# One value scale per head group, applied in the copies; the prompt's neighbourhood planes made one step later

## The chip, the cores and the metric

One core of one Trainium2 chip runs the whole kernel. The metric is the device time of one execution in microseconds (us); what is compared are medians of several executions. The profile and the trace come from one execution, recorded by the hardware profiler. Its engines are called PE (TensorE, the matrix engine), PEld (its weight loads), DVE (VectorE), ACT (ScalarE), POOL (GpSimd) and SP (SyncE, which here only issues DMAs).

## The reference

One encoder layer is applied to two inputs, x_prompt (1024 tokens) and x_sample (512 tokens), both 1024 wide:

```
xn = RMSNorm(x);  z = xn @ W_in -> q_A k_A v_A q_B k_B v_B gate_A gate_B
o_A = softmax(q_A k_A^T / 8) v_A     # 8 query heads share 2 key/value heads; RMS-normed, rotated q and k
o_B = softmax(q_B k_B^T / 8 + bias) v_B   # 8 heads, a clamped 8 x 16 window on a token grid 64 wide
mix = (sigmoid(gate_A) * (o_A @ W_pA) + sigmoid(gate_B) * (o_B @ W_pB)) @ W_out
x = x + mix;  x = x + relu(RMSNorm(x) @ W_up)^2 @ W_down;  y = RMSNorm(x)
```

Everything is float32, and the outputs must be close to a float32 computation.

## The kernel before

**Precision.** A float32 product is made of three matmuls on operands that are split into a high and a low part (mm3, lines 242 to 245). In the prompt's attention, the probabilities and the values are kept as two float16 planes, high and low, of a number that was scaled into the range of float16. The probabilities are scaled by the constant PSC. The values are scaled column by column; the scales are worked out from the weights, as a bound on the largest value that a column can give (value_scales, lines 180 to 204).

**Stages.** The sample (s0) goes first, then the prompt (s1), each through: the projections of branch A for key/value group 0 (phR), grouped attention of that group (phA), the same for group 1, neighbourhood attention (phB, branch B), the output projections (phG). The profiled execution has them at, in us: s0 projections 0 to 50 and 93 to 127, grouped attention 50 to 93 and 127 to 170, neighbourhood attention 170 to 320, outputs 320 to 390; s1 projections 390 to 460 and 575 to 650, grouped attention 460 to 575 and 650 to 760, neighbourhood attention 760 to 1065, outputs 1065 to 1250. The MLP of both inputs fills the rest.

**Order.** A scheduler puts each engine's instructions in a row from the order of the code and its own estimate of lengths; some instructions are pinned to the order of the code. At run time each engine works its row off strictly, waiting for semaphores. The matmuls of the gates are cut into pieces ("fill", outputs gpss) and are put between the others wherever the code calls fill.pull, so that PE has work while other engines prepare its operands. DMAs are issued mostly by SP, in a row as well.

**The value scales before.** During the sample's neighbourhood attention, a block of 128 weight columns (raw, one of three shared load buffers called rawvs here) is loaded per step. DVE takes the absolute value (aw, line 197), PE multiplies it with a matrix of the norm's weights (gm) in eight matmuls (line 200), which gives the 128 sums on every partition; DVE adds a tiny number (line 202), takes the inverse (sv, line 203), and ACT's queue writes the row to DRAM (vsc). This is done for five blocks. The prompt's stages read vsc back: broadcast over partitions as svb and svv for the projections (lines 667 to 669), as a column inv for grouped attention (lines 862 to 867) and as iv for neighbourhood attention (lines 1041 to 1047).

**The uses before.** In the prompt's projections, values() lets DVE scale the projected values of branch B (vs, line 712), ACT round them to the high plane and DVE subtract for the low one (vt). rotate() does the same for branch A's values with DVE (line 796), ACT, and POOL for the difference (line 802). In grouped attention, s_tile() takes the inverse of the row sum (rl, line 891, DVE), multiplies it by PSC (rc, line 893, POOL), and makes the planes hl of the probabilities.

**Neighbourhood attention of the prompt.** There are 32 units (8 heads by 4 column blocks), one per step of a loop; fill is pulled twice a step. s_unit() makes a unit's scores in two halves (matmuls sbs, line 1153; both halves lie in one PSUM tile). Per half, DVE adds the bias and mask (bms, made by POOL) and takes the row's maximum in one instruction, which the trace names msbs and sbss (line 1155); ACT takes the exponential (pbs, line 1159); DVE the inverse sum (rsbs, line 1162); POOL multiplies it by PSC (line 1167); ACT makes the high plane (hbs, line 1170) and DVE the low one (line 1171). SP issues a DMA that transposes both planes into bhs (line 1176). There are three buffers of hbs, one per half, and three of bhs. Two steps after the scores, v_unit() multiplies bhs with the values (obs, line 1220), and ACT and DVE scale the result back by iv (lines 1227 and 1228, output os_B).

## Time and profile before

| what | us |
|---|---|
| median of three runs | 2134.73 |
| fastest of the three | 2132.63 |
| the profiled execution's own time | 2130.55 |
| its span in the trace | 2128.7 |
| POOL busy | 351.5 (17%) |
| ACT busy | 1138.2 (53%) |

The span is what the trace covers from first to last instruction; the 1.85 us beside it belong to the start and end of the execution. The mean granted clock of PE is 0.996. A row of a group of instructions names the line, the engine, the operation, what it writes and reads, and minimum, median and maximum in ns. A row of waits names who waited, for whom, the us in total, how many times, and the longest. An event has its start and length, and in brackets how long the engine stood idle before it and what released it.

### The profile page before, as it was taken

Reading aid. Unit: us, or ns where it says so; the run is one execution under the profiler, and the core shown is the slowest. Engines: PE = TensorE matmul, PEld = TensorE weight load, DVE = VectorE, ACT = ScalarE, POOL = GpSimd, SP = SyncE. Lnnn points to the kernel's source line nnn. Section 1 sums busy time; section 2 is a strip of 40 time slices with the busy share of each in tenths; the row PEclk is TensorE's granted clock in tenths of the full one; section 3 lists DMA queues with packets and bytes.
Section 4 is the critical chain, followed back from the end, with each engine's and each line's share of the span. In section 5 each row is a group of like instructions: output and inputs, shape, how many; then the busy total and the mean of one; then the engine's idle time right before and its main releaser. Section 6 shows DMA issues by size and latency. Waiting matters only on the chain.

```text
span 2128.7 us, 31427 instructions
## 1 busy us (share of the span) xinstructions
PE 2078.9 (98%) x10559; PEld 1784.9 (84%) x10559; DVE 1498.4 (70%) x2848; ACT 1138.2 (53%) x2352; POOL 351.5 (17%) x588
## 2 busy tenths in 40 slices
PE   9999899999999999999999999999999999999998
PEld 8887778987797777776788999999999988888887
DVE  6675777778767855667772877778777777659563
ACT  5664454657636755566531566666565633434352
POOL 3332330432242222332101200003000000000000
PEclk9999999999999999999999999999999999999999
DMA  6445647634525556655772666478544799688561
GB/s 189 135 125 155 181 151 260 214 83 103 116 59 127 119 123 130 163 125 133 196 246 102 209 197 200 154 247 210 159 148 157 260 354 341 214 277 275 176 198 69
DMA packets 446582, 376.94 MB, mean 177 GB/s; under 512 B 169158, under 2 KB 384083, under 8 KB 446420
## 3 DMA queue, kind: packets, MB, share of 16 engines
q1 hardware_dynamic: 404471, 307.00, 49.4%
q10 hardware_dynamic: 36268, 50.88, 7.1%
q0 software_dynamic: 5680, 17.04, 2.9%
q8 instruction: 83, 1.36, 0.3%
q14 instruction: 80, 0.65, 0.1%
HBM read 263.62 MB, written 85.79 MB: 164 GB/s over the span
## 4 chain that ended last, share of the span: by engine, by line
PE 49%; DVE 1%; issue 1%; DMA 0%; POOL 0%; ACT 0%; POOLq 0%; ACTq 0%; DVEq 0%
PE dn L243 7%; PE dn L245 7%; PE dn L244 7%; PE uc L243 2%; PE uc L244 2%; PE ud L244 2%; PE ud L243 2%; PE ud L245 2%; PE uc L245 2%; PE ua L245 2%; PE ua L244 2%; PE ua L243 2%; PE ops L244 1%; PE ops L243 1%; PE ops L245 1%; PE ub L244 1%
## 5 line engine op out<-in xcount | busy, mean ns | idle before, releaser
L245 PE MATMUL dn<-wd,al 128*128 128x512 f32 (+1 forms) x624 | 242.3, 388 | 0.0
L244 PE MATMUL dn<-wd,ah 128*128 128x512 f32 (+1 forms) x624 | 242.3, 388 | 0.0
L243 PE MATMUL dn<-wd,ah 128*128 128x512 f32 (+1 forms) x624 | 242.3, 388 | 0.0
L1524 ACT ACTIVATE ah<-ar 128x512 fp32r<-128x512 f32 x168 | 104.4, 627 | 201.8 <-PE dn L244 181.0
L1525 DVE TENSOR_TENSOR al<-ar,ah 128x512 fp32r<-128x512 f32 x168 | 115.1, 693 | 74.6 <-ACT ah L1524 66.6
L245 PEld LDWEIGHTS dn<-wd,al 128*128 128x128 f32 x624 | 117.1, 188 | 24.4
L243 PEld LDWEIGHTS dn<-wd,ah 128*128 128x128 f32 x624 | 117.1, 188 | 24.1
L244 PEld LDWEIGHTS dn<-wd,ah 128*128 128x128 f32 x624 | 117.1, 188 | 24.1
L880 DVE TENSOR_REDUCE nms<-ss 128x1 f32<-128x1024 f32 (+1 forms) x96 | 99.5, 1038 | 12.0 <-PE ss L878 11.6
L883 ACT ACTIVATE ps<-ss,nms 128x1024 f32<-128x1024 f32 (+1 forms) x96 | 93.0, 970 | 24.1 <-DVE nms L880 9.3
L243 PE MATMUL gpss<-xs_0h,w_gs 128*128 128x512 f32 x256 | 102.8, 402 | 2.1 <-DVE ptls L919 1.3
L228 POOL TENSOR_TENSOR rs_f<-ms_f,mhalf 128x1 f32<-128x1 f32 x6 | 4.0, 667 | 590.7 <-DVE ms_f L224 590.7
L245 PE MATMUL gpss<-xs_0h,w_gs 128*128 128x512 f32 x256 | 100.8, 394 | 0.2 <-DVE w_gs L238 0.2
L244 PE MATMUL gpss<-xs_0l,w_gs 128*128 128x512 f32 x256 | 100.8, 394 | 0.0
L1524 ACT ACTIVATE A<-S 128x512 fp32r<-128x512 f32 x128 | 76.1, 624 | 30.9 <-DVE S L1587 26.5
L1525 DVE TENSOR_TENSOR A<-S,A 128x512 fp32r<-128x512 f32 x128 | 84.5, 686 | 3.8 <-ACT A L1524 3.8
L1643 ACT ACTIVATE c<-c 128x384 f32<-128x384 f32 x97 | 50.7, 524 | 67.9 <-DVE c L1642 67.9
L243 PE MATMUL uc<-B,A 128*128 128x384 f32 x256 | 85.6, 334 | 0.2 <-ACT s L1659 0.2
L243 PE MATMUL ud<-B,A 128*128 128x384 f32 x256 | 85.6, 334 | 0.0
L245 PE MATMUL ud<-B,A 128*128 128x384 f32 x256 | 85.5, 334 | 0.0
L244 PE MATMUL ud<-B,A 128*128 128x384 f32 x256 | 85.5, 334 | 0.0
L244 PE MATMUL uc<-B,A 128*128 128x384 f32 x256 | 85.5, 334 | 0.0
(393 smaller groups left out, 6340.8 us busy)
## 6 DMA issues: line engine op xcount, KB each, us to landing
ar<-ud SPq DMA_DIRECT2D x120, 512.0 KB
br<-in_w_mlp_down_dram SPq DMA_DIRECT2D x72, 512.0 KB
rawu<-in_w_mlp_up_dram SPq DMA_DIRECT2D x64, 512.0 KB
ud<-c ACTq DMA_DIRECT2D x128, 192.0 KB
raw_gs<-in_w_in_dram SPq DMA_DIRECT2D x32, 512.0 KB
zgs<-sgs ACTq DMA_DIRECT2D x48, 256.0 KB
ud<-cs SPq DMA_DIRECT2D x64, 192.0 KB
vss<-vds SPq DMA_DIRECT2D x256, 32.0 KB
```

The source lines that it names most:

```text
L228: nc.gpsimd.tensor_tensor(r[:, :n], m[:, :n], mhalf[:, :n], op=ALU.pow)
L243: nc.tensor.matmul(out, ah, bh, start=start, stop=False, **kw)
L244: nc.tensor.matmul(out, ah, bl, start=False, stop=False, **kw)
L245: nc.tensor.matmul(out, al, bh, start=False, stop=stop, **kw)
L880: nc.vector.tensor_reduce(nm_, s, axis=AX.X, op=ALU.max, negate=True)
L883: nc.scalar.activation(p, s, AF.Exp, bias=nm_, accum_out=l)
L1524: nc.scalar.activation(hi, src, AF.Copy)
L1525: nc.vector.tensor_tensor(lo, src, hi.bitcast(F32), op=ALU.subtract)
L1643: nc.scalar.activation(t, t, AF.Relu)
```

## The change

It has four parts.

1. There is one scale for each of four groups of columns (branch A's two key/value heads, and heads 0 to 3 and 4 to 7 of branch B) instead of one per column. It is the sum over the rows of the weights of the largest absolute weight of a row in that group, times the norm's weight. DVE finds the row maxima in five reductions; a single matmul of 128x4 against a constant matrix adds them over the partitions. All is done in the sample's second projection, and the scales stay on the chip in svs; vsc and the DMAs that wrote and read it are gone. The columns of svs are used as a per-partition scalar.
2. In the prompt's projections ACT scales while it copies from PSUM, and DVE makes the low plane from PSUM in one instruction (values, rotate).
3. In grouped attention of the prompt DVE scales the row sum by 1/PSC ahead of its inverse; POOL's multiply is gone, and so is one link of the chain.
4. In the prompt's neighbourhood attention the inverse sums, the planes and the transposes of a unit are a function of their own, planes(), called at the start of the next step. DVE scales both halves' sums in one instruction and inverts them in another; POOL's two multiplies are gone.

```diff
@@ value_scales
-        for b, off in enumerate((640, 1792, 1920, 2048, 2176)):
...
-            nc.sync.dma_start(rv, win[:, off : off + P].rearrange("(k p) c -> p k c", p=P))
-            yield
...
-            nc.vector.scalar_tensor_tensor(aw, rv, -1.0, rv, op0=ALU.mult, op1=ALU.max)
...
-            for k in range(NC8):
-                nc.tensor.matmul(pt, gm[:, k, :], aw[:, k, :], start=(k == 0), stop=(k == NC8 - 1))
...
-            nc.vector.tensor_scalar(sv, pt, 1e-30, None, op0=ALU.add)
-            nc.vector.reciprocal(sv, sv)
-            nc.scalar.dma_start(vsc[:, b * P : (b + 1) * P], sv[0:1, :])
...
+        blocks = ((640, 2, 0), (1792, 1, 0), (1792, 1, 1), (2048, 1, 0), (2048, 1, 1))
...
+        for b in range(3):
+            load(b)
+        yield
+        for b, (off, nh, kb) in enumerate(blocks):
...
+            nc.vector.tensor_reduce(
+                dst.rearrange("p h k -> p k h") if nh == 2 else dst,
+                rv.rearrange("p k (h d) -> p k h d", d=HD) if nh == 2 else rv,
+                axis=AX.X,
+                op=ALU.max,
+                apply_absolute_value=True,
+            )
+            if b + 3 < 5:
+                load(b + 3)
+            if b < 4:
+                yield
...
+        nc.vector.tensor_tensor(top, top, ga.to_broadcast([P, 4, NC8]), op=ALU.mult)
+        nc.vector.tensor_reduce(svs[:, 8:12], top, axis=AX.X, op=ALU.add)
+        yield
+        pt = mm("vs")[:, 0:4]
+        nc.tensor.matmul(pt, ones, svs[:, 8:12], start=True, stop=True)
+        nc.vector.tensor_scalar(svs[:, 4:8], pt, 1e-30, None, op0=ALU.add)
+        nc.vector.reciprocal(svs[:, 0:4], svs[:, 4:8])
+        nc.vector.tensor_scalar(svs[:, 4:8], svs[:, 4:8], 1.0 / PSC, None, op0=ALU.mult)
@@ values
-                        nc.vector.tensor_tensor(vs, zv4, svv.rearrange("p (h d) -> p h d", d=HD), op=ALU.mult)
-                        nc.scalar.activation(vt[:, :, 0:HD], vs, AF.Copy)
-                        nc.vector.tensor_tensor(vt[:, :, HD:P], vs, vt[:, :, 0:HD], op=ALU.subtract)
+                        sv = svs[:, 2 + g : 3 + g]
+                        nc.scalar.activation(vt[:, :, 0:HD], zv4, AF.Copy, scale=sv)
+                        nc.vector.scalar_tensor_tensor(
+                            vt[:, :, HD:P], zv4, sv, vt[:, :, 0:HD], op0=ALU.mult, op1=ALU.subtract
+                        )
@@ rotate
-                            nc.vector.tensor_tensor(vr, z[:, 320:384], svb, op=ALU.mult)
...
-                            nc.scalar.activation(hi, vr, AF.Copy)
-                            nc.gpsimd.tensor_tensor(lo, vr, hi if tt >= NP else hi.bitcast(F32), op=ALU.subtract)
+                            sv = svs[:, g : g + 1]
+                            nc.scalar.activation(hi, z[:, 320:384], AF.Copy, scale=sv)
+                            nc.vector.scalar_tensor_tensor(
+                                lo, z[:, 320:384], sv, hi if tt >= NP else hi.bitcast(F32),
+                                op0=ALU.mult, op1=ALU.subtract,
+                            )
@@ grouped attention, s_tile
-                    nc.vector.tensor_scalar(inv, inv, PSC, None, op0=ALU.mult)
-                    nc.vector.reciprocal(inv, inv)
+                inv = svs[:, 4 + g : 5 + g] if ND else None
...
-                    nc.vector.reciprocal(rl, l)
...
-                    nc.gpsimd.tensor_scalar(rlc, rl, PSC, 1.0, op0=ALU.mult, op1=ALU.mult)
+                    nc.vector.tensor_scalar(l, l, 1.0 / PSC, None, op0=ALU.mult)
+                    nc.vector.reciprocal(rlc, l)
...
-                    nc.gpsimd.tensor_scalar(pn, p[:, 0 : NP * P], rl, PSC, op0=ALU.mult, op1=ALU.mult)
+                    nc.gpsimd.tensor_scalar(pn, p[:, 0 : NP * P], rlc, 1.0, op0=ALU.mult, op1=ALU.mult)
@@ neighbourhood attention, s_unit and planes
-                    nc.vector.reciprocal(rl[:, x : x + 1], l[:, x : x + 1])
...
-                    nc.gpsimd.tensor_scalar(rlc, rl[:, x : x + 1], PSC, 1.0, op0=ALU.mult, op1=ALU.mult)
...
-                    nc.scalar.activation(h2[:, :, 0, :], pv3, AF.Copy, scale=rlc)
...
+            def planes(u):
...
+                nc.vector.tensor_scalar(l[:, 0:2], l[:, 0:2], 1.0 / PSC, None, op0=ALU.mult)
+                nc.vector.reciprocal(rl[:, 0:2], l[:, 0:2])
...
+                for hf in range(2):
...
+                    nc.scalar.activation(h2[:, :, 0, :], pv3, AF.Copy, scale=r_)
                     nc.vector.scalar_tensor_tensor(
-                        h2[:, :, 1, :], pv3, rlc, h2[:, :, 0, :], op0=ALU.mult, op1=ALU.subtract
+                        h2[:, :, 1, :], pv3, r_, h2[:, :, 0, :], op0=ALU.mult, op1=ALU.subtract
                     )
...
                     nc.sync.dma_start_transpose(
...
@@ v_unit
-                    nc.scalar.activation(t, o[HD:P], AF.Copy, scale=iv[HD:P, h : h + 1])
...
+                    nc.scalar.activation(t, o[HD:P], AF.Copy, scale=svs[HD:P, 6 + h // 4 : 7 + h // 4])
...
@@ the loop over the units
+                if JN == 1 and 0 < i <= n:
+                    planes(units[i - 1])
                 if i < n:
                     s_unit(units[i])
...
-                if i >= 3:
-                    next(vsg, None)
```

How the rows of the engines change is shown at three places. Numbers after a name tell buffers apart; sbss1_2_1_0 is the prompt's head 2, column block 1, half 0.

DVE in the prompt's neighbourhood attention, around the units (2, 1) and (2, 2), before (ISA is the reduction of the scores, with its second part that reads the maximum out; hbs are the low planes, os_Bs an output):

```order
L1155 ISA sbss1_2_1_0_9804,msbs1_2_1_9797<-sbs1_2_1_9795,bms1_2_1_0_9800 128x384
L1155 ISA msbs1_2_1_9797 128x1
L1155 ISA sbss1_2_1_1_9818,msbs1_2_1_9797<-sbs1_2_1_9795,bms1_2_1_1_9814 128x384
L1155 ISA msbs1_2_1_9797 128x1
L1162 RECIPROCAL rsbs1_2_1_9799<-ssbs1_2_1_9798 128x1
L1171 SCALAR_TENSOR_TENSOR hbs1_2_1_0_9809<-pbs1_2_1_9796,rsbs1_2_1_9799,hbs1_2_1_0_9809 128x3x128
L1162 RECIPROCAL rsbs1_2_1_9799<-ssbs1_2_1_9798 128x1
L1155 ISA sbss1_2_2_0_9895,msbs1_2_2_9890<-sbs1_2_2_9888,bms1_2_1_0_9800 128x384
L1155 ISA msbs1_2_2_9890 128x1
L1171 SCALAR_TENSOR_TENSOR hbs1_2_1_1_9823<-pbs1_2_1_9796,rsbs1_2_1_9799,hbs1_2_1_1_9823 128x3x128
L1228 SCALAR_TENSOR_TENSOR os_Bs1_1_0_9883<-obs1_1_0_9877,ivs1_8935,ot_Bs1_1_0_9882 64x512
```

The same place in the changed kernel:

```order
L1166 ISA sbss1_2_1_0_9590,msbs1_2_1_9583<-sbs1_2_1_9581,bms1_2_1_0_9586 128x384
L1166 ISA msbs1_2_1_9583 128x1
L1166 ISA sbss1_2_1_1_9597,msbs1_2_1_9583<-sbs1_2_1_9581,bms1_2_1_1_9593 128x384
L1166 ISA msbs1_2_1_9583 128x1
L1184 TENSOR_SCALAR ssbs1_2_1_9584<-ssbs1_2_1_9584 128x2
L1185 RECIPROCAL rsbs1_2_1_9585<-ssbs1_2_1_9584 128x2
L1192 SCALAR_TENSOR_TENSOR hbs1_2_1_0_9664<-pbs1_2_1_9582,rsbs1_2_1_9585,hbs1_2_1_0_9664 128x3x128
L1192 SCALAR_TENSOR_TENSOR hbs1_2_1_1_9668<-pbs1_2_1_9582,rsbs1_2_1_9585,hbs1_2_1_1_9668 128x3x128
L1166 ISA sbss1_2_2_0_9679,msbs1_2_2_9674<-sbs1_2_2_9672,bms1_2_1_0_9586 128x384
L1166 ISA msbs1_2_2_9674 128x1
L1245 SCALAR_TENSOR_TENSOR os_Bs1_1_0_9656<-obs1_1_0_9650,svs_95,ot_Bs1_1_0_9655 64x512
L1166 ISA sbss1_2_2_1_9684,msbs1_2_2_9674<-sbs1_2_2_9672,bms1_2_1_1_9593 128x384
```

The inverse of the first half, which stood between a unit's planes and reductions, is gone from there; one multiply and one inverse for both halves stand ahead of both low planes, and both low planes stand ahead of the next unit's first reduction here.

DVE at the start of the sample's second projection, before (ms_As is the mean square that POOL takes the root of, ts the normed queries and keys):

```order
L224 TENSOR_SCALAR ms_As0_1_0_1292<-ssAs0_1_0_1286 128x5
L789 SCALAR_TENSOR_TENSOR ts0_1_0_1296<-zs0_1_0_1260,rs_As0_1_0_1294,gtab_93 128x64 x5
L805 TENSOR_TENSOR vhls0_1_1257<-zs0_1_0_1260,vhls0_1_1257 128x64
L224 TENSOR_SCALAR ms_As0_1_1_1345<-ssAs0_1_1_1339 128x5
L789 SCALAR_TENSOR_TENSOR ts0_1_1_1349<-zs0_1_1_1313,rs_As0_1_1_1347,gtab_93 128x64 x5
L805 TENSOR_TENSOR vhls0_1_1257<-zs0_1_1_1313,vhls0_1_1257 128x64
L819 TENSOR_TENSOR ts0_1_0_1296<-ts0_1_0_1296,rts0_1_0_1258 128x320
L826 TENSOR_TENSOR rrs0_1_0_1308<-ts0_1_0_1296,us0_1_0_1304 128x320
```

And in the changed kernel:

```order
L207 TENSOR_REDUCE vtop_1262<-rawvs0_1263 128x8x2
L247 TENSOR_SCALAR ms_As0_1_0_1303<-ssAs0_1_0_1297 128x5
L207 TENSOR_REDUCE vtop_1262<-rawvs1_1265 128x4
L811 SCALAR_TENSOR_TENSOR ts0_1_0_1307<-zs0_1_0_1271,rs_As0_1_0_1305,gtab_93 128x64 x5
L207 TENSOR_REDUCE vtop_1262<-rawvs2_1267 128x4
L829 TENSOR_TENSOR vhls0_1_1257<-zs0_1_0_1271,vhls0_1_1257 128x64
L247 TENSOR_SCALAR ms_As0_1_1_1362<-ssAs0_1_1_1356 128x5
L811 SCALAR_TENSOR_TENSOR ts0_1_1_1366<-zs0_1_1_1330,rs_As0_1_1_1364,gtab_93 128x64 x5
L829 TENSOR_TENSOR vhls0_1_1257<-zs0_1_1_1330,vhls0_1_1257 128x64
L219 SCALAR_TENSOR_TENSOR gc_1258<-gc_1258 128x8
```

Three of the five reductions of weights (vtop) now stand among the first tiles' norm and rotation, the first of them ahead of the first mean square.

SP's row in the same stage, before (raw_gs are the loads of gate weights):

```order
L268 DMA raw_gs0_2304_4_0_1455<-in_w_in_dram 128x8x128
L268 DMA raw_gs0_2304_5_0_1621<-in_w_in_dram 128x8x128
L268 DMA raw_gs0_2304_6_0_1692<-in_w_in_dram 128x8x128
L220 DMA biases_97<-shifted_96 128x768
L742 DMA rts0_1_0_1258<-in_rope_dram 128x128
L742 DMA rts0_1_1_1311<-in_rope_dram 128x128
L742 DMA rts0_1_2_1364<-in_rope_dram 128x128
L220 DMA biases_97<-shifted_96 128x768
L742 DMA rts0_1_3_1461<-in_rope_dram 128x128
L268 DMA raw_gs0_2304_7_0_1820<-in_w_in_dram 128x8x128
```

And in the changed kernel:

```order
L196 DMA rawvs0_1263<-in_w_in_dram 128x8x128
L196 DMA rawvs1_1265<-in_w_in_dram 128x4x256
L196 DMA rawvs2_1267<-in_w_in_dram 128x4x256
L243 DMA biases_98<-shifted_97 128x768
L184 DMA gc_1258<-in_norm_mix_g_dram 128x8x1
L764 DMA rts0_1_0_1269<-in_rope_dram 128x128
L196 DMA rawvs3_1323<-in_w_in_dram 128x4x256
L196 DMA rawvs4_1326<-in_w_in_dram 128x4x256
L764 DMA rts0_1_1_1328<-in_rope_dram 128x128
L764 DMA rts0_1_2_1382<-in_rope_dram 128x128
L291 DMA raw_gs0_2304_4_0_1474<-in_w_in_dram 128x8x128
L764 DMA rts0_1_3_1480<-in_rope_dram 128x128
```

The five loads of value weights stand ahead of the gate weights 4 to 7 and use the same three buffers.

More of the change, by code (lines that the diff above doesn't have):

```diff
@@ L115, in encoder @@
     gtab = cst.tile([P, 5, HD], F32, name="gtab")
-    mhalf = cst.tile([P, 48], F32, name="mhalf")
+    mhalf = cst.tile([P, 8], F32, name="mhalf")
+    svs = cst.tile([P, 40], F32, name="svs")
     nc.vector.memset(mhalf, -0.5)
@@ L119, in encoder @@
     biases = dram.tile([8, 16, 8, 16, 48], F32, name="biases")
-    vsc = dram.tile([1, 640], F32, name="vsc")
     def row_bcast(dst, src, n, rep=1):
@@ L188, in value_scales @@
[L188 to L204 removed]
+        ones = pool.tile([P, P], F32, tag="vone", name="vone", bufs=1)
@@ new lines, in value_scales, with load @@
+        nc.gpsimd.memset(ones, D**0.5 / VTOP)
+        top = pool.tile([P, 4, NC8], F32, tag="vtop", name="vtop", bufs=1)
+        blocks = ((640, 2, 0), (1792, 1, 0), (1792, 1, 1), (2048, 1, 0), (2048, 1, 1))
+        raws = {}
+        def load(b):
+            off, nh, kb = blocks[b]
+            ncol = P if nh == 2 else 256
+            raw = rawp.tile([P, 1024], F32, tag="raw", name=f"rawvs{b}")
+            raws[b] = raw.rearrange("p (k c) -> p k c", c=ncol)
+            nc.sync.dma_start(
+                raws[b],
+                win[kb * 512 : kb * 512 + 1024 * P // ncol, off : off + ncol].rearrange("(k p) c -> p k c", p=P),
+            )
@@ L665, in run @@
                 if ND:
-                    svb = ph.tile([P, HD], F32, tag="svb", name=f"svb{N}_{g}", bufs=1)
-                    nc.sync.dma_start(svb, vsc[:, g * HD : g * HD + HD].to_broadcast([P, HD]))
-                    svv = ph.tile([P, 4 * HD], F32, tag="svv", name=f"svv{N}_{g}", bufs=1)
-                    nc.sync.dma_start(svv, vsc[:, P + g * 256 : P + g * 256 + 256].to_broadcast([P, 256]))
                     vpl = vps.tile([P, ND, 2, HD], F16, tag="vp", name=f"vpl{N}_{g}", bufs=1)
+                vsg = value_scales(ph) if first and g == 1 else iter(())
+                next(vsg, None)
                 rr_of = {}
@@ L832, in run @@
                         flush_heads()
+                    next(vsg, None)
+                    if tt == 0:
+                        next(vsg, None)
                     t_ = r0 + tt
@@ L850, in run @@
                 fill.pull(6)
+                next(vsg, None)
                 heads_t(NT - 1)
@@ L1039, in run @@
             JN = 3 - halves
-            if JN == 1:
-                iv = ph.tile([P, 8], F32, tag="iv", name=f"iv{N}", bufs=1)
-                for e in range(2):
-                    nc.sync.dma_start(
-                        iv[e * HD : e * HD + HD], vsc[:, P : P + 512].rearrange("o (h d) -> d (o h)", d=HD)
-                    )
-                nc.vector.tensor_scalar(iv, iv, PSC, None, op0=ALU.mult)
-                nc.vector.reciprocal(iv, iv)
             msk = ph.tile([P, halves * 3, nkey], BF16, tag="msk", name=f"msk{N}", bufs=1)
             nc.gpsimd.dma_start(msk, w["mask2"] if halves == 2 else w["mask1"])
-            rects, strips, bms, PT = {}, {}, {}, {}
+            rects, strips, bms, PT, rls = {}, {}, {}, {}, {}
             def prep(h):
@@ L1257, in v_unit @@
                 nc.vector.tensor_tensor(lo, b0, hi.bitcast(F32), op=ALU.subtract)
-            vsg = value_scales(ph) if first else iter(())
             prep(0)
```

50 lines of the change are left out of this document (20 added, 30 removed).

## The prediction

> **What bounds the kernel now.** I read the busy times first, then the stages, then the waits of the engine that bounds. The first lines of the page:
> ```profile
> span 2128.7 us, 31427 instructions
> PE 2078.9 (98%) x10559; PEld 1784.9 (84%) x10559; DVE 1498.4 (70%) x2848; ACT 1138.2 (53%) x2352; POOL 351.5 (17%) x588
> ```
> TensorE (PE) is busy for 2078.9 of 2128.7 us, so all its pauses together are 2128.7 − 2078.9 = 49.8 us. The change can gain only what it takes out of TensorE's own work, out of these pauses, and out of time at a lowered clock. Busy time per stage shows where the pauses lie (columns: window, length, busy PE, PEld, DVE, ACT, POOL, clock, DMA share, GB/s):
> ```profile
> 130.00:320.00 190.00, 181.92 (x912) 145.71 (x911) 132.04 (x318) 106.67 (x221) 60.13 (x89) 1.00 0.55 159
> 460.00:575.00 115.00, 110.80 (x543) 83.89 (x541) 93.27 (x147) 85.04 (x144) 30.23 (x64) 1.00 0.51 111
> 650.00:760.00 110.00, 107.27 (x516) 78.18 (x514) 89.93 (x138) 83.61 (x140) 26.71 (x61) 1.00 0.51 114
> 760.00:1065.00 305.00, 285.48 (x1264) 218.73 (x1264) 194.17 (x481) 170.69 (x332) 82.57 (x145) 0.98 0.62 147
> ```
> These are the neighbourhood attention of the sample (8.1 us of pauses), the two grouped attentions of the prompt (4.2 and 2.7) and the neighbourhood attention of the prompt (19.5). The change touches these four and the projections; all after 1065 us stays. What TensorE waits for, from 130 to 320 us (first row) and from 760 to 1065 us (the other three):
> ```profile
> PE sbs L1153 <- DVE msbs L1155: 5.0, 8, 1.4
> ...
> PE sbs L1153 <- DVE msbs L1155: 14.9, 18, 2.6
> PE sbs L1153 <- DVE rsbs L1162: 2.4, 1, 2.4
> PE obs L1220 <- DMA bhs<-hbs: 1.6, 1, 1.6
> ```
> In the prompt's stage 14.9 + 2.4 = 17.3 us are score matmuls (sbs) that wait until VectorE (DVE) has reduced the scores before them (msbs). DVE is busy for only 194.17 of 305 us there, so it isn't short of time; it stands still in its row. The longest such wait but two, event by event (the last row is TensorE):
> ```profile
> 872.57 0.62 ACT L1170 ACTIVATE hbs<-pbs,rsbs 128x384 f16<-128x384 f32 x1 [1.48 <-DMA bhs<-hbs]
> 873.22 0.62 DVE L1171 SCALAR_TENSOR_TENSOR hbs<-pbs,rsbs,hbs 128x384 f16<-128x384 f32 x1 [1.48 <-ACT hbs L1170]
> 873.93 0.74 DVE L1228 SCALAR_TENSOR_TENSOR os_Bs<-obs,ivs,ot_Bs 64x512 f32<-64x512 f32 x1
> 874.60 0.54 DVE L1155 CUSTOM_DVE_ANT_0 sbss<-sbs,bms 128x384 f32<-128x384 f32 x1
> 875.20 0.62 PE L1153 MATMUL sbs<-kBs,qBs 128*128 128x384 f32 x2 [2.00 <-DVE msbs L1155]
> ```
> ScalarE (ACT) waits 1.48 us for a plane buffer, DVE's low plane waits behind ACT, the reduction stands behind that, and TensorE waits 2.00 us. The links over the whole stage:
> ```profile
> DVE hbs L1171 <- ACT hbs L1170: 32.1, 32, 3.5
> ACT hbs L1170 <- POOL rsbs L1167: 30.6, 29, 2.6
> POOL rsbs L1167 <- DVE rsbs L1162: 45.6, 27, 12.7
> DVE rsbs L1162 <- ACT pbs L1159: 12.6, 12, 1.7
> ```
>
> **The scales (value_scales).** Their price before: TensorE's own time in the windows that hold all 40 matmuls of line 200, and DVE's three operations per block.
> ```profile
> sum 44.00, PE 5.49 PEld 5.39; mean PE 1.10 PEld 1.08
> L197 DVE SCALAR_TENSOR_TENSOR aw<-rawvs x5: 1207/1220/1255, 206.1 to 249.5; 128x1024 fp32r<-128x1024 f32 x5
> L202 DVE TENSOR_SCALAR sv<-vs x5: 272/277/292, 217.0 to 256.0; 128x128 f32<-128x128 f32 x5
> L203 DVE RECIPROCAL sv<-sv x5: 929/953/953, 218.4 to 258.8; 128x128 f32<-128x128 f32 x5
> ```
> The 40 matmuls took 5.49 us of an engine that has no slack: −5.5. The one new matmul, 128x4, is not in the trace; it lies between 0 and one block of eight (5.49 / 5 = 1.1); nearest is a single matmul of such a block, 0.14, with its weight load and a turn of PSUM I take +0.3. ACT loses one copy of 128x1024; DVE loses 5 × (1.220 + 0.277 + 0.953) = 12.3 us between 206 and 260 us, where it is busy for 69% (132.04 of 190) and holds TensorE up for part of the 5.0 us above. The bounds are 0 and −8.1 (every pause of the stage); I take −2, two fifths of those waits. The five loads go to an earlier stage.
>
> There, in the second projection of the sample at 93 to 130 us, DVE gets five reductions. The nearest row is a reduction of the same kind and size (below it the fullest window of 5 us, and the sum of the eight windows from 90 to 130 us):
> ```profile
> L880 DVE TENSOR_REDUCE nms<-ss x96: 666/1206/1225, 52.3 to 750.5; 128x1 f32<-128x1024 f32 x64, 128x1 f32<-128x512 f32 x32
> 120.00:125.00 5.00, 5.00 (x31) 4.43 (x31) 4.85 (x12) 2.63 (x7) 1.68 (x3) 1.00 0.41 147
> sum 40.00, PE 40.00 PEld 37.44 DVE 24.31 ACT 17.18 POOL 11.96; mean PE 5.00 PEld 4.68 DVE 3.04 ACT 2.15 POOL 1.49
> ```
> 5 × 1.21 and six small ones at about 0.15 (a small one is priced below) make 7.0 us. TensorE has no pause there (40.00 of 40), and DVE is busy for 24.31 of 40, so the cover is 15.7 us, but little of it from 120 to 125 us. The first reduction stands ahead of the group's first mean square, so a late load would hold up the rotation, and POOL's root, which waits for that. On SP's queue the five loads stand ahead of the next gate weights' (w_gs 4 to 7), and all go through the same three buffers, so these weights are split later. Bounds 0 and +7.0; I take +1, since three loads are asked for at the stage's start.
>
> **Scales in the copies.** Per tile of the prompt's projections DVE loses the scaled copies of lines 712 and 796; POOL's subtraction becomes one on DVE:
> ```profile
> L712 DVE TENSOR_TENSOR vss<-zvs,svvs x16: 404/416/423, 406.4 to 641.0; 128x256 f32<-128x256 f32 x16
> L796 DVE TENSOR_TENSOR ts<-zs,svbs x16: 205/214/225, 403.5 to 637.9; 128x64 f32<-128x64 f32 x16
> PE gpss L243 <- DVE vss L712: 0.7, 1, 0.7
> ```
> DVE: −16 × (0.416 + 0.214) + 16 × about 0.22 = −6.6 us, spread over 145 us in which TensorE hardly pauses. One pause of 0.7 us hangs on line 712; bounds −1 and +0.5 (the copy now reads PSUM), taken −0.5. Fifteen small DMAs on the SP and ACT queues and the inversions of inv and iv go; no row of TensorE's waits names them: 0.
>
> **Grouped attention of the prompt.** Of 64 tiles each, DVE gets a multiply, POOL loses one:
> ```profile
> L893 POOL TENSOR_SCALAR rcs<-rls x64: 190/192/553, 465.0 to 754.0; 128x1 f32<-128x1 f32 x64
> L866 DVE TENSOR_SCALAR invs<-invs x2: 135/144/154, 464.8 to 650.0; 128x1 f32<-128x1 f32 x2
> PE pTs L914 <- POOL pns L904: 1.3, 2, 0.9
> ...
> PE pTs L914 <- POOL pns L904: 0.4, 2, 0.2
> ```
> DVE: +64 × 0.144 = +9.2 us in 225 us, where it is busy for 93.27 + 89.93 = 183.2 us already (81%, then 85%). A hop of 0.19 us to POOL goes out of each tile's path, at a price of 0.144. Bounds: −1.7 (TensorE's waits for POOL's pns, 460 to 575 us and 650 to 760) and +9.2; I take +1, near cover, since the tile's work has lead over its use and the hop falls away.
>
> **Planes one step later.** Per unit of the prompt's neighbourhood attention two reciprocals and two POOL multiplies
> ```profile
> L1162 DVE RECIPROCAL rsbs<-ssbs x96: 135/162/168, 184.7 to 1047.3; 128x1 f32<-128x1 f32 x96
> L1167 POOL TENSOR_SCALAR rsbs<-rsbs x64: 180/190/624, 790.6 to 1047.5; 128x1 f32<-128x1 f32 x64
> ```
> become one multiply and one reciprocal of two columns: 2 × 0.162 against 0.144 + 0.162, so nothing in DVE's busy time. What moves is the row. In the row before, the reduction of a unit's second half stands behind the reciprocal of its first half, which waits for ACT's exponential, in 13 of the 32 units; in the new row in none. The link to POOL (30.6 us of ACT's waiting) falls away, and with it the 45.6 us in which POOL's multiply stood waiting at the head of its queue, ahead of mask sums (bms) and output moves (os_B). But the two low planes still stand ahead of the next unit's first reduction in 15 of 31 places (18 before), still wait for ACT (32.1 us), and ACT still waits for plane buffers, of which there are three as before. The two transposes of a unit go onto SP's queue as a pair and, in the code, one step of 9.5 us (305 / 32) later, while the product with the values stays two steps behind the scores: one step of lead is left, for a transfer that TensorE has waited 1.6 us for (obs). I take a third of the 17.3 us, −6; bounds 0 and −17.3.
>
> Some of the pauses were followed by a lowered clock:
> ```profile
> 1000.00:1010.00 10.00, 9.04 (x27) 5.83 (x28) 6.91 (x18) 5.50 (x12) 3.41 (x6) 0.66 0.85 228
> 1030.00:1040.00 10.00, 7.42 (x28) 5.59 (x28) 7.65 (x19) 5.90 (x14) 3.44 (x6) 0.83 0.67 177
> 1000.14 1.07 PE L1153 MATMUL sbs<-kBs,qBs 128*128 128x384 f32 x4 [2.35 <-DVE rsbs L1162]
> ```
> That is 10 × 0.34 + 10 × 0.17 = 5.1 us lost, once right behind a pause of 2.35 us on the very reciprocal that is moved. I take half: −2.5 (bounds 0 and −5.1). The Trainium skill, page "TensorE: Matmul & The Clock Gate", section "What's actually happening", has the clock halve only after an idle window of about 3.4 us; no single pause here is so long, so the row shows a cluster of shorter pauses doing it. By that rule alone the clock would not be the change's to win, and the sum would be 2.5 us higher.
>
> **Sum** against the profiled execution's own 2130.55 us: −5.5 + 0.3 − 2 + 1 − 0.5 + 1 − 6 − 2.5 = −14.2, so 2116.4. The median shown, 2134.73, is 4.2 above that execution and the fastest run, 2132.63, is 2.1 above; I add 2.6: **2119**, with 2110 to 2127 as this case's own range.
>
> **Rivals.** (A) *The waits stay, moved.* The low planes still hold the reductions up, through ACT and the plane buffers (the event list above began with a DMA, not with POOL). Then only the matmuls go: 2130.55 − 5.2 + 2.6 = 2128. For it: the 32.1 us on ACT and 15 places against 18. Against it: 13 places to none. (B) *Slower.* Both planes of a unit now wait for its second exponential, and together run 0.144 + 0.162 + 3 × 0.62 (ACT's and DVE's planes in the event list), some 2.2 us, before the next unit's first reduction in those 15 places. It decides where TensorE has less than exponential plus planes plus reduction, some 0.6 + 2.2 + 0.6 = 3.4 us (exponential and reduction each taken as long as a plane), of filling work between two units' scores. If all 15 gain a wait of the mean seen, 14.9 / 18 = 0.83, and the old ones stay: +12.4 − 5.2, or 2140. For it: a step near the end has little filling work. Against it: a step has 9.5 us on the mean. (C) *Nearly all goes*: 17.3 + 5.1 + 5.5 − 0.3 + 5, or 32.6 less: 2101. Against it: the three buffers.
>
> **How the numbers follow.** Chances: forecast 0.50, A 0.22, B 0.16, C 0.12. From 2103 to 2137 leaves out most of C and about half of B: two in ten at most. Two per cent, about what a measurement of this kernel can tell from no change, is 43 us: faster needs under 2092, for which C and nearly every other pause would have to go (0.02); slower needs over 2177, about four times B's new waits (0.02).
>
> **What would show it.** Right: TensorE's busy time down by some 5 us; TensorE's waits for msbs near 9 us in the prompt's stage, with the clock rows nearer 1.00; no new pause at 93 to 130 us. Wrong: as many waits for msbs with ACT or a transpose ahead (A, B), pauses on w_gs at 115 to 130 us, or on the grouped attention's tiles.

## The result

The changed kernel takes 2106.5 us (median of four runs, 2104.4 to 2109.4) against 2132.6 us for the kernel before (median of three runs, 2130.2 to 2134.7; a fourth run, of 2553 us, is far from all others and is left out). The ratio is 0.988, with a 95% interval of 0.986 to 0.990: 26 us or 1.2% less. That is less than the two per cent that the prediction took as about what a measurement can tell from no change, though the interval is clear of 1. Of the prediction's two ranges, 2106.5 lies in the wide one (2103 to 2137) and outside the narrow one (2110 to 2127); it is 12.5 us below the forecast of 2119. Between the profiled executions, 2130.55 and 2107.3 us, 23.2 us were gained, where the terms add up to 14.2.

The first lines of the page of the changed kernel:

```profile
span 2105.5 us, 31206 instructions
PE 2071.3 (98%) x10521; PEld 1783.3 (85%) x10521; DVE 1500.9 (71%) x2885; ACT 1137.8 (54%) x2351; POOL 330.4 (16%) x445
```

The span is 23.2 us shorter. PE's busy time fell by 7.6 us, its pauses by 15.6 (from 49.8 to 2105.5 − 2071.3 = 34.2). So two thirds of the gain are pauses. To see where, the two traces are cut at the same events, not at the same times. The rows are the sample's neighbourhood attention (from its first score matmul to the first matmul of the next stage), the second grouped attention of the prompt (from the last transposed query to the last product with the values), and the prompt's neighbourhood attention (from the first score matmul to the last product with the values). First the kernel before:

```profile
180.60:318.30 137.70, 130.27 (x659) 105.12 (x659) 101.07 (x249) 75.71 (x156) 44.52 (x67) 1.00 0.56 163
642.20:762.70 120.50, 117.60 (x562) 85.69 (x561) 94.63 (x147) 88.93 (x149) 28.25 (x64) 1.00 0.53 122
785.80:1056.60 270.80, 251.45 (x1116) 191.56 (x1115) 176.88 (x439) 158.02 (x311) 77.64 (x139) 0.98 0.63 147
```

The same three of the changed kernel:

```profile
181.20:307.40 126.20, 124.20 (x620) 100.60 (x620) 90.38 (x234) 75.80 (x156) 46.42 (x67) 1.00 0.53 158
629.30:747.20 117.90, 115.92 (x563) 86.47 (x562) 97.42 (x176) 88.29 (x149) 24.01 (x32) 1.00 0.60 131
770.00:1033.30 263.30, 250.24 (x1114) 191.41 (x1114) 184.14 (x439) 158.33 (x311) 68.88 (x75) 0.99 0.65 150
```

The second number of a row is the length. The sample's neighbourhood attention lost 11.5 us, 6.1 of it busy time and 5.4 pauses. The second grouped attention lost 2.6. The prompt's neighbourhood attention lost 7.5, of which 6.3 are pauses. That is 21.6 of 23.2. Of the rest, the stretch from the prompt's first transposed query to its first grouped score lost 3.3 (52.7 to 49.4 us) and the first grouped attention 0.8 (136.0 to 135.2), while the output stage of the sample got 2.2 longer (87.6 to 89.8).

PE's waits for the reductions in the two neighbourhood attentions of the changed kernel, the sample's in the first row, and below them what DVE and ACT wait for in the prompt's:

```profile
PE sbs L1164 <- DVE msbs L1166: 0.8, 3, 0.4
...
DVE ssbs L1184 <- ACT pbs L1170: 25.5, 20, 1.9
...
PE sbs L1164 <- DVE msbs L1166: 12.7, 15, 3.8
DVE hbs L1192 <- ACT hbs L1191: 10.5, 20, 0.8
...
ACT hbs L1191 <- DMA bhs<-hbs: 4.6, 7, 1.4
```

The sample's 5.0 us are nearly gone (0.8). Of the prompt's 17.3 us, 12.7 stay, although DVE's waits for ACT's planes fell from 32.1 to 10.5 and ACT's for POOL's multiply are gone. DVE still stands still in its row: it now waits 25.5 us for ACT's exponentials ahead of the inverse, where it waited 12.6 before. The longest wait grew, from 2.6 to 3.8. Around it, event by event (PE's last row, the others DVE):

```profile
1001.85 1.15 DVE L1192 SCALAR_TENSOR_TENSOR hbs<-pbs,rsbs,hbs 128x384 f16<-128x384 f32 x2
1003.43 0.69 DVE L261 TENSOR_TENSOR oXs<-rawos,oXs 128x512 fp32r<-128x512 f32 x1 [0.43 <-ACT oXs L255]
1004.03 0.68 DVE L1047 SCALAR_TENSOR_TENSOR mAs<-zas,ppas 128x512 f32<-128x512 f32 x1
1004.63 0.55 DVE L1166 CUSTOM_DVE_ANT_0 sbss<-sbs,bms 128x384 f32<-128x384 f32 x1
...
1005.25 0.73 PE L1164 MATMUL sbs<-kBs,qBs 128*128 128x384 f32 x2 [3.77 <-DVE msbs L1166]
```

The scores of this reduction had been there since 1000.5 us; DVE first worked off, among others, both low planes, a split of the attention's output and a gate product. The clock over the windows of 10 us that show less than 1.00:

```profile
970.00:980.00 10.00, 7.62 (x34) 5.68 (x32) 7.92 (x22) 6.78 (x16) 6.04 (x7) 0.92 0.47 106
980.00:990.00 10.00, 10.00 (x44) 7.36 (x43) 9.42 (x22) 5.24 (x11) 2.27 (x3) 0.91 1.07 237
1000.00:1010.00 10.00, 6.23 (x22) 4.89 (x21) 8.46 (x19) 5.98 (x13) 3.21 (x4) 0.83 0.57 157
```

That is 0.8 + 0.9 + 1.7 = 3.4 us lost, against 5.1 before. And the sample's second projection with its five new reductions (the sum of the eight windows from 90 to 130 us, and the reductions):

```profile
sum 40.00, PE 40.00 PEld 37.87 DVE 27.68 ACT 18.09 POOL 11.56; mean PE 5.00 PEld 4.73 DVE 3.46 ACT 2.26 POOL 1.45
```
```profile
L207 DVE TENSOR_REDUCE vtop<-rawvs x5: 1202/1210/1214, 96.1 to 114.5; 128x4 f32<-128x1024 f32 x4, 128x16 f32<-128x1024 f32 x1
```

PE has no pause there, as before. A reduction takes 1.21 us, as estimated.

### The profile page after: what moved, and what is told of

Read it like the earlier page. It is cut to its first block, busy times and chain, and to the rows that moved or that the text cites. A ratio compares the mean times of both kernels' runs of the same rounds, so it can differ in the third digit from the quotient of the medians.

```text
span 2105.5 us, 31206 instructions
## 1 busy us (share of the span) xinstructions
PE 2071.3 (98%) x10521; PEld 1783.3 (85%) x10521; DVE 1500.9 (71%) x2885; ACT 1137.8 (54%) x2351; POOL 330.4 (16%) x445
## 4 chain that ended last, share of the span: by engine, by line
PE 52%; DVE 1%; issue 1%; DMA 1%; ACT 1%; SPq 0%; POOL 0%; ACTq 0%; POOLq 0%; DVEq 0%
PE dn L267 7%; PE dn L268 7%; PE dn L266 7%; PE uc L266 2%; PE ud L266 2%; PE uc L268 2%; PE ud L268 2%; PE ud L267 2%; PE uc L267 2%; PE ua L266 2%; PE ua L268 2%; PE ua L267 2%; PE ops L267 1%; PE ops L268 1%; PE ops L266 1%; PE ub L266 1%
## 5 line engine op out<-in xcount | busy, mean ns | idle before, releaser
L1150 POOL TENSOR_TENSOR bms<-rects,msks 128x384 f32<-128x384 f32 (+1 forms) x72 | 64.2, 896 | 154.6 <-DVE msbs L1166 114.5
L1170 ACT ACTIVATE pbs<-sbss,msbs 128x384 f32<-128x384 f32 (+1 forms) x96 | 55.3, 577 | 58.8 <-POOL os_Bs L1263 23.3
L266 PE MATMUL ud<-B,A 128*128 128x384 f32 x256 | 85.7, 335 | 0.0
```

The costliest lines, as they stand in the source:

```text
L266: nc.tensor.matmul(out, ah, bh, start=start, stop=False, **kw)
L1150: nc.gpsimd.tensor_tensor(bm.rearrange("p (r c) -> p r c", c=32), rects[h][:, ir : ir + kr_n, jr : jr + 32], msk[:, hf * 3 + ct, :].rearra ...
L1170: nc.scalar.activation(p[:, x], sb, AF.Exp, bias=nm_[:, x : x + 1], scale=-1.0, accum_out=l[:, x : x + 1])
```

## The experiments

Twelve kernels were run, most of them the changed kernel with one part undone. Medians of one call are compared with runs of the kernel before on the same chip, which gave 2129 to 2131 us; the changed kernel itself was not timed again beside them. Two medians of different calls that lie within some 3 us of each other are therefore not told apart, and what follows goes by the length of the stage in the trace, where an undisturbed stage repeats better. How well differs: the last 1072 us were 1071.6 to 1073.9 long in all traces, the sample's neighbourhood attention was 126.0 to 126.2 in the four kernels that leave it alone, the start up to it 179.5 to 181.9, and the prompt's neighbourhood attention 261.4 to 264.4 in the changed kernel (263.3) and the six others that leave it alone. So in this last stage a difference of less than 3 us from single traces says nothing.

### Planes in their own step

The call of planes() stands behind s_unit() of the same step:

```diff
-                if JN == 1 and 0 < i <= n:
-                    planes(units[i - 1])
                 if i < n:
                     s_unit(units[i])
+                    if JN == 1:
+                        planes(units[i])
```

> The changed kernel (2106.5 us), but planes() called right behind s_unit() of the same step, not one step later; DVE still scales and inverts both halves' sums at once. Theory 1: what gains is that the inverse sums are taken once per unit behind both reductions, without POOL; the scheduler lays the rows nearly alike, so the time stays within 3 us of 2106.5 and TensorE's waits for msbs in the prompt's neighbourhood attention stay near 12.7 us. Theory 2 (the later step itself gains): those 7 us come back, 2113 to 2115, with msbs waits near 17.

Measured: 2111.5 us, ratio 0.991 (0.989 to 0.992). The prompt's neighbourhood attention takes 268.6 us, 5.3 more than the changed kernel, and PE waits 16.2 us for reductions; 5.1 us are lost at a lowered clock there, against 3.4. Theory 1 falls, in the stage as in the waits. Theory 2 is near in the waits (17), though the time stays under its 2113 to 2115. DVE's row differs in few places: both low planes of a unit stand ahead of the next unit's first reduction in 20 of 31 places, against 15 in the changed kernel and 18 in the kernel before. Here is one between the third and the fourth unit (rows of ACT, DVE and PE):

```profile
783.26 0.61 ACT L1191 ACTIVATE hbs<-pbs,rsbs 128x384 f16<-128x384 f32 x1 [2.20 <-DMA bhs<-hbs]
...
783.91 0.62 DVE L1192 SCALAR_TENSOR_TENSOR hbs<-pbs,rsbs,hbs 128x384 f16<-128x384 f32 x1 [2.12 <-ACT hbs L1191]
784.44 0.55 DVE L1166 CUSTOM_DVE_ANT_0 sbss<-sbs,bms 128x384 f32<-128x384 f32 x1
...
785.06 0.62 PE L1164 MATMUL sbs<-kBs,qBs 128*128 128x384 f32 x2 [2.62 <-DVE msbs L1166]
```

ACT waits 2.20 us until a transpose has freed a plane buffer. The low plane waits behind ACT, and the next unit's reduction stands behind the low plane. In the changed kernel that reduction stands ahead of it, and PE's waits around this place are 0.36 and 0.57 us. So the later step does pay, and in this place it pays through the place of the low plane in DVE's row; that the other places work alike was not followed.

### POOL's multiply kept

```diff
-                nc.vector.tensor_scalar(l[:, 0:2], l[:, 0:2], 1.0 / PSC, None, op0=ALU.mult)
-                nc.vector.reciprocal(rl[:, 0:2], l[:, 0:2])
+                for x in range(2):
+                    nc.vector.reciprocal(rl[:, x : x + 1], l[:, x : x + 1])
+                    nc.gpsimd.tensor_scalar(rl[:, 4 + x : 5 + x], rl[:, x : x + 1], PSC, 1.0, op0=ALU.mult, op1=ALU.mult)
```

> The changed kernel, but in planes() one inverse per half by DVE and POOL's multiply by PSC behind each, as before. Theory 1: the chain through POOL comes back: ScalarE waits some 30 us for POOL again, and the time rises by 3 to 8 us (2110 to 2115). Theory 2 (the later step gains): within 2 us of 2106.5. Rival A of the prediction (buffers and ScalarE hold the row up, POOL does not matter): within 2 us as well, with ScalarE's waits shifted from POOL to the transposes.

Measured: 2103.6 us, ratio 0.987 (0.986 to 0.989), the stage 261.1 us, 2.2 less than in the changed kernel and within the spread of that stage. What POOL, ACT and PE wait for in it:

```profile
POOL rsbs L1186 <- DVE rsbs L1185: 40.6, 26, 14.1
...
ACT hbs L1192 <- POOL rsbs L1186: 4.9, 9, 1.6
...
PE sbs L1164 <- DVE msbs L1166: 11.0, 15, 1.7
PE sbs L1164 <- DVE rsbs L1185: 1.9, 1, 1.9
```

POOL stands waiting at the head of its queue for 40.6 us again (45.6 in the kernel before), and PE's waits are 12.9 us, as without it. ACT's planes wait only 4.9 us for it, not the some 30 us of theory 1, so with the later step the chain through POOL has mostly gone by itself. Within the spread, moving the multiply to DVE won nothing.

### The tiles of grouped attention, and the copies, as before

In the first of these two kernels s_tile() has the inverse by DVE and the multiply by POOL again; in the second, values() and rotate() scale by DVE first (now with a column of svs), then round, then subtract:

```diff
-                    nc.vector.tensor_scalar(l, l, 1.0 / PSC, None, op0=ALU.mult)
-                    nc.vector.reciprocal(rlc, l)
+                    nc.vector.reciprocal(rl, l)
...
+                    nc.gpsimd.tensor_scalar(rlc, rl, PSC, 1.0, op0=ALU.mult, op1=ALU.mult)
```

> The changed kernel, but grouped attention's tiles of the prompt with the inverse by DVE and POOL's multiply, as before. If the hop through POOL cost time there: the two grouped attentions together become 2 to 4 us longer (2109 to 2110), mostly the second. If the 3 to 4 us gained between 458 and 763 us came from elsewhere (the copies, or DMAs that are gone): within 1 us of 2106.5, or 1 us faster, since DVE has 64 multiplies less.

```diff
-                        nc.scalar.activation(vt[:, :, 0:HD], zv4, AF.Copy, scale=sv)
+                        nc.vector.tensor_scalar(vs, zv4, sv, None, op0=ALU.mult)
+                        nc.scalar.activation(vt[:, :, 0:HD], vs, AF.Copy)
...
-                            nc.scalar.activation(hi, z[:, 320:384], AF.Copy, scale=sv)
+                            nc.vector.tensor_scalar(vr, z[:, 320:384], sv, None, op0=ALU.mult)
+                            nc.scalar.activation(hi, vr, AF.Copy)
```

> The changed kernel, but in the prompt's projections DVE scales the values first (now by a column of svs), ScalarE rounds and DVE or POOL subtracts, as before. By the prediction's term: +0.5 us (2107). If the copies account for the gain before the prompt's neighbourhood attention: +2 to +4 us (2109 to 2110), visible between the first projection and the last os matmul.

Measured: 2106.7 us (ratio 0.989, 0.987 to 0.991) and 2106.8 us (0.989, 0.987 to 0.991); as whole times both are inconclusive. In the traces each shows in one stage. With the old tiles the second grouped attention takes 119.9 us:

```profile
626.60:746.50 119.90, 116.18 (x563) 86.26 (x562) 94.13 (x144) 88.95 (x149) 28.07 (x64) 1.00 0.59 125
```

It is 117.4 to 118.4 us long in the eleven kernels with the new tiles (the changed one among them), and 120.5 and 121.4 in the two that have the old code throughout. So about 2 us are the new tiles', though DVE is busier by 3.3 us with them. The first grouped attention doesn't show it (134.8 us from its first score matmul to the next projection's first transpose, against 135.2), and couldn't: it is 134.3 to 138.7 long in the kernels that leave it alone. With the old copies, the stretch from the prompt's first transposed query to its first grouped score takes 51.0 us, with 1.8 of pauses; it takes 49.4 to 49.7 with 0.5 to 0.8 in all kernels that have the new copies, and 52.7 in the kernel before. So 1.6 of the 3.3 us gained there are the copies'; the other 1.7 were not traced to a part of the change.

### What the old scales cost

Four kernels share the question of the 11.5 us. The first has the new scales, but worked out in the old place, a block a step in the sample's neighbourhood attention:

```diff
-                vsg = value_scales(ph) if first and g == 1 else iter(())
-                next(vsg, None)
+                vsg = iter(())
...
+            vsg = value_scales(ph) if first else iter(())
...
+                if i >= 3:
+                    next(vsg, None)
```

> The changed kernel with its new, cheap scales worked out in the sample's neighbourhood attention, one block per step from the fourth step on, where the old ones were. If the gain there (137.7 to 126.2 us) came from the work that is gone: within 1.5 us of 2106.5, that stage 126 to 128 us. If it came from the place: that stage takes 130 us or more and the time is 2110 or more.

The second is the changed kernel that does the old work there too (called osg here) and doesn't use it:

```diff
+            osg = old_scales(ph) if first else iter(())
...
+                if i >= 3:
+                    next(osg, None)
```

> The changed kernel, and the old column scales are worked out as well in their old place (their result is written to DRAM and not used): 5 loads, 15 DVE operations, 40 matmuls. Both theories: the stage goes back by about 11.5 us, the time to about 2118; the sum of its two parts is what the next two runs split. If the stage's gain was something else (another order of the row): +6 us or less.

The third has of each block's eight matmuls only the first:

```diff
-            for k in range(NC8):
-                nc.tensor.matmul(pt, gm[:, k, :], aw[:, k, :], start=(k == 0), stop=(k == NC8 - 1))
+            nc.tensor.matmul(pt, gm[:, 0, :], aw[:, 0, :], start=True, stop=True)
```

> As the run before, but with one matmul of each eight (5 instead of 40): loads and DVE's work alone, 12.3 us of DVE. Prediction's term (two fifths of the waits hang on DVE): +2 us and the five matmuls' 0.7, 2109. If DVE's row accounts for all pauses that went from the stage: +5 to +6 us, 2112, with TensorE's waits for msbs near 5 us.

The fourth has the 40 matmuls, without loads and without DVE's work:

```diff
-                nc.tensor.matmul(pt, gm[:, k, :], aw[:, k, :], start=(k == 0), stop=(k == NC8 - 1))
+                nc.tensor.matmul(pt, gm[:, k, :], gm[:, (k + 1) % NC8, :], start=(k == 0), stop=(k == NC8 - 1))
...
+            nc.scalar.activation(sv[0:1, :], pt[0:1, :], AF.Copy)
```

> The changed kernel with 40 matmuls of 128x128 on an operand that is ready since the stage's start, ScalarE taking out one row of the result; no loads, no DVE work. What TensorE's own time of the matmuls is worth: +5.5 us by the rows (2112). If part of it fits into pauses: +3 us or less. The output does not depend on them.

Measured: 2109.3, 2117.4, 2112.7 and 2112.1 us; ratios 0.991 (0.990 to 0.993), 0.995 (0.993 to 0.996), 0.992 (0.991 to 0.994) and 0.992 (0.990 to 0.993). The stage in the four traces, in this order, each row from a trace of its own:

```profile
181.50:313.00 131.50, 126.64 (x622) 102.11 (x622) 96.43 (x244) 75.47 (x156) 44.90 (x67) 0.99 0.58 171
```
```profile
180.50:317.50 137.00, 131.11 (x659) 106.52 (x659) 100.98 (x248) 75.46 (x156) 46.01 (x67) 0.99 0.56 165
```
```profile
181.10:312.80 131.70, 126.06 (x624) 101.36 (x624) 100.38 (x250) 75.78 (x156) 47.55 (x68) 1.00 0.59 173
```
```profile
179.70:312.20 132.50, 128.97 (x659) 105.20 (x659) 90.50 (x234) 76.75 (x161) 43.33 (x67) 1.00 0.51 151
```

Against 126.2 us, the old work costs 10.8, near the 11.5 that were expected. Its matmuls alone cost 6.3, of which 4.8 are busy time. Its loads and DVE work with five matmuls cost 5.5; with 0.7 for these five (5.49 / 40 each), 4.8 remain. The parts add up to 11.1, though 1.7 of the 10.8 are a lowered clock that neither part shows. What the parts cost is clear; by which wait is another matter. PE's waits for the reductions of the scores, in the third kernel and then in the fourth:

```profile
PE sbs L1190 <- DVE msbs L1192: 1.3, 3, 0.6
```
```profile
PE sbs L1185 <- DVE msbs L1187: 3.2, 6, 1.1
```

They are 0.8 us in the changed kernel, 3.6 in the second of these four and 5.0 in the kernel before. So the loads and DVE's work hardly bring them back (1.3, where near 5 was expected if DVE's row made them); the matmuls alone, with no work for DVE, bring more. The pauses of the third kernel are mostly on other operands, none longer than 0.8 us. The new scales, with half of DVE's work (five reductions of 1.21 us against 12.3 us), cost 5.3 us in the same place, as much as the old ones' loads and DVE work; 1.7 of the 5.3 are a lowered clock behind the longest pause. PE's pauses there were 4.9 us, and they weren't waits for the reductions of the scores; the largest named ones:

```profile
PE pkbs L266 <- DVE bhs L1214: 1.8, 1, 1.8
PE sbs L1163 <- DVE msbs L1165: 1.1, 3, 0.4
```

So for the new scales the second expectation holds in the stage (130 us or more), while the time, 2109.3, is just under its 2110: the place counts. Whether the loads, which share three buffers with other weights, or DVE's operations do the harm there was not tried apart.

### A PSUM tile for each half

In the code, both halves of a unit's scores lie in one PSUM tile. The waits that stay in the prompt's stage are all of score matmuls for reductions, and a reduction is no input of a score matmul. Counted through the trace, 14 of the 15 waits (11.1 of 12.7 us) stand ahead of a unit's second half, and 18 of 19 (16.4 of 17.3) in the kernel before. This kernel gives each half a tile of its own out of the same two buffers:

```diff
-                s = big(f"sb{N}_{h}_{js[0]}")
...
-                    so = s[:, x * 512 : x * 512 + nkey]
+                    so = big(f"sb{N}_{h}_{j}_{hf}")[:, 0:nkey]
```

> The changed kernel, but each half of a unit's scores in neighbourhood attention gets a PSUM tile of its own from the same two buffers, so that the second half's matmul no longer writes the tile that VectorE still reads the first half from. Theory: the remaining 12.7 us of waits for msbs in the prompt's stage are waits of the second half for the first half's reduction; they fall to 4 us or less, the clock stays at 1.00, and the time falls by 8 to 15 us (2092 to 2098). Rival: VectorE's row is late anyway, and the next unit's first half waits in its place: waits near 12 us, within 3 us of 2106.5.

The same edit was made to the kernel before, alone:

> The kernel before with the same edit alone. Theory: its 17.3 us of waits on the reductions in the prompt's stage fall to 5 us or less, and part of the sample's 5.0 us, with the lowered clock of 5.1 us: 2112 to 2120. If the waits hang on the chain through POOL and ScalarE: within 4 us of 2133.7.

Measured: 2094.0 us (five runs, 2093.7 to 2094.4), ratio 0.983 (0.981 to 0.984), and 2111.3 us, ratio 0.991 (0.989 to 0.992). Both theories hold in the main, though the clock doesn't stay at 1.00 (0.83 in one window of 10 us of the first kernel and 0.66 in one of the second), and the second keeps 6.9 us of waits where 5 or less were expected. In the sample's neighbourhood attention no wait for a reduction is left in either; of the 5.0 us, the kernel before with the edit alone gains only 2.4 (135.3 us against 137.7), as 3.4 are lost there at a lowered clock. With the change and the edit the prompt's neighbourhood attention takes 252.8 us, 10.5 less; PE's waits for the reductions there fall from 12.7 to 3.9 us:

```profile
766.50:1019.30 252.80, 244.80 (x1115) 191.96 (x1114) 181.40 (x439) 157.37 (x311) 70.72 (x75) 0.99 0.67 155
```
```profile
PE sbs L1163 <- DVE msbs L1165: 3.9, 4, 1.6
PE obs L1236 <- DMA bhs<-hbs: 3.3, 2, 2.4
```

The kernel before with the edit alone shows, in the same stage:

```profile
786.70:1040.30 253.60, 245.99 (x1115) 192.18 (x1114) 175.49 (x436) 156.29 (x310) 77.92 (x138) 0.99 0.65 153
```
```profile
DVE hbs L1170 <- ACT hbs L1169: 35.4, 28, 2.7
ACT hbs L1169 <- POOL rsbs L1166: 34.0, 27, 2.5
...
PE sbs L1152 <- DVE msbs L1154: 6.9, 8, 2.1
```

This is the clearest pair of the study. The chain from POOL over ACT to DVE is as long as it was (34.0 and 35.4 us of waits, against 30.6 and 32.1), and yet the stage is 17.2 us shorter and as short as with the change (253.6 against 252.8). The chain reached PE mostly because the second half's matmul had to wait until the first half had been read out of the shared tile.

### The half tiles with other parts undone

> The changed kernel with one PSUM tile per half and, besides, planes() in the unit's own step. Theory: with the shared tile gone, a low plane that is laid ahead of a reduction no longer holds TensorE, so the step of the planes is worth little: within 2 us of 2094.0, or up to 3 us less, since the transposes go out earlier and TensorE's two waits for them (0.9 and 2.4 us) shrink. Rival: the later step gains by itself: the 5.3 us come back, 2098 to 2100.

> The changed kernel with one PSUM tile per half and POOL's multiply by PSC kept. Theory: the hop through POOL is hidden: within 2 us of 2094.0. Rival: it was hidden only by the waits that the half tiles took away, and shows now: 2097 or more.

The edits are those shown above, together. Measured: 2099.5 us, ratio 0.986 (0.984 to 0.988), and 2094.3 us, ratio 0.983 (0.982 to 0.985). With POOL's multiply the stage is 253.4 us: hidden, as expected. With the planes in their own step it is 257.2, 4.4 more, and the time lies in the rival's 2098 to 2100:

```profile
768.10:1025.30 257.20, 247.88 (x1115) 192.34 (x1115) 179.05 (x439) 157.66 (x311) 66.39 (x75) 0.99 0.67 154
```
```profile
1015.94 0.61 ACT L255 ACTIVATE w_pas<-raw_pas 128x512 fp32r<-128x512 f32 x1
...
1016.61 0.50 PE L266 MATMUL ppas<-oXs,w_pas 128*128 128x512 f32 x1 [2.13 <-ACT w_pas L255]
```

One new pause of 2.13 us stands near the end, on a weight that ACT splits late. Another 3 us are busy time (247.88 against 244.80), 1.0 of it a lowered clock that falls just behind the stage's end in the other kernel. The kernel with half tiles alone shows 2.4 us of waiting for a transpose instead. The waits for reductions, by which the step was thought to pay, are 4.7 us against 3.9. And the kernel before with half tiles, whose planes stand in their own step too, takes 253.6. So the time speaks against the theory, but not by the rival's path; which part belongs to the step and which to the row that the scheduler happened to lay is not settled by one trace.

## Why the prediction was right or wrong

**The matmuls (−5.5 + 0.3).** Right in size: put back alone, they cost 6.3 us of the stage, 4.8 of it busy time. The other 1.5 are pauses that the term did not have: 3.2 us of waits for reductions come back with them.

**DVE's relief in the sample's neighbourhood attention (−2).** Mis-sized, and by a path that the runs don't bear out. PE's pauses of the stage went from 7.4 to 2.0 us and its waits for reductions from 5.0 to 0.8, not by two fifths; the bound of 8.1 held. But the loads and DVE's work, put back, cost 4.8 us with only 1.3 us of such waits. And half tiles alone take all of these waits away with DVE's work still in place. So by these traces the loads and DVE's work did not cost their 4.8 us by holding up the reductions; most of it lies in small pauses on other operands, and whether loads or DVE caused them stays open.

**The new place of the scales (+1).** Mis-sized, no cost is seen. The cover named for it (PE without a pause from 90 to 130 us, 15.7 us free on DVE) was enough. What the working left out is what the place is worth: the same new work costs 5.3 us where the old work stood.

**The copies (−0.5).** The sign was right and the size too low: 1.6 us in the stretch where the old copies show, outside the bound of −1. Another 1.7 us of that stretch went with no term to account for them. The small DMAs and inversions that were put at 0 are a candidate; no run puts them back.

**Grouped attention (+1).** The sign was wrong: −2.6 us in the second grouped attention, about 2 of it due to the new tiles, where the bound was −1.7 for both attentions. The 9.2 us more on DVE were counted as a possible loss, and the hop that falls away as cover for it; the traces show a small gain and no loss from DVE's load. That the gain comes through the hop is argued from the edit, not shown by a wait.

**The planes (−6, clock −2.5).** The sum was near: −7.5 where −8.5 was forecast. Of the waits 4.6 us went, and 1.7 at the clock (5.1 to 3.4); the 12.7 us that stay are more than the sign of being right, near 9. The reason was right only in part. Of the three things that were named, the link to POOL is worth nothing beside the later step (it can be put back), and the count of reductions behind their own unit's inverse explains little, since the kernel with planes in their own step has none of them either and gives 5.3 of the 7.5 us back. What fits is how often the low planes, which wait for ACT as ACT does for a buffer, are laid ahead of the next unit's first reduction: 18 places before, 20 in their own step, 15 in the changed kernel. The prediction had 15 against 18 and made little of them. But with a tile for each half the count loses its weight: the kernel before has 23 such places then, in 253.6 us.

**The step that was missing.** The prediction took it as given that a score matmul waits for "the scores before them" to be reduced, and didn't ask why. The answer, one PSUM tile for two halves, was in the code. It bounds what the planes' step can win, and it is worth more than the step: 17.2 us of the stage alone.

**Rivals.** A said that the waits would stay, moved: 12.7 of 17.3 us did stay, while the time fell through other terms. B's place is there, the 3.77 us behind both low planes, but no other wait in the stage is longer than 1.6. C, at 2101, was nearer to the measured time than the forecast, yet by another way than C's: the prompt's waits didn't go.

**The scale.** 2.6 us were added for the difference of the profiled execution to the medians. The median of 2134.73 that this leaned on counts the run of 2553 us; the other three runs have a median of 2132.6, 2.1 above the profiled execution. The changed kernel's profiled execution lies 0.8 above its median, so 3.4 of the 12.5 us missed are spread between executions.

**The sum.** The other 9 us or so are the terms'. The sample's neighbourhood attention gave 4.3 us more than its three parts, the grouped attentions 4.4 more, the copies' stretch 2.8 more; the planes gave 1.0 less, and the sample's output stage, which no term touched, took 2.2. That the time lies in the wide range is owed to its width more than to the sum.

## What to carry to other kernels

When an engine with no slack waits for a consumer to read something, ask first which buffer it wants; a tile that two producers share makes the second one wait for the first one's reader, and a tile for each can be worth more than shortening the reader's chain. Work on a second engine is priced by where it stands: 6 us of reductions with their loads cost 5.3 us in one stage, and in a stage where the bounding engine has no pause no cost is seen. Before costing a move by counts in a row, find the few places where an instruction that waits for a third engine stands ahead of one that the bounding engine needs.

## What was not expected of the hardware

The clock fell below 1.00 after pauses of very different lengths. In the changed kernel it stood at 0.92 and 0.91 from 970 to 990 us, after pauses of 1.52 and 0.86 us within two microseconds, while the single pause of 3.77 us was followed by 0.83 over 10 us. The Trainium skill's page "TensorE: Matmul & The Clock Gate", section "What's actually happening", ascribes the lowered clock to an idle window of about 3.4 us; apart from the 3.77 us, no pause named here is so long.

The prediction read the lowered clock as the work of a cluster of pauses. That is not needed either. Three pauses that stood alone were each followed by about 1.7 us lost at the clock: 2.58 us in the kernel before (at 1034.7 us, the 0.83 that the prediction shows), 1.83 us with the new scales in the old place, and 1.41 us with the old work put back. One of 2.62 us, in the kernel with planes in their own step at 785 us, was followed by none. What decides is open.
